# Value blocks multiplied in pairs, as products of 512 columns, for five token groups

## The chip, the cores and the metric

One core of a Trainium2 chip runs the whole layer as one program. The metric is the device time of that core in microseconds, the median of several executions. A profiled execution of the same program gives the rows below.

## The reference, cut to what matters

The input x has 2048 tokens of 1024 channels. A norm with shift and scale from the vector c gives h, and one product with `w_in` gives all projections:

```python
h = rmsnorm(h_res, norm_w[l]) * (1.0 + scale[:, None, :]) + shift[:, None, :]
proj = h @ w_in + b_in
(na_q, na_k, na_v, na_z, ml_q, ml_k, ml_v, ml_o, ml_z, i_f, f_f, i_b, f_b) = jnp.split(proj, split_idx, axis=-1)
```

`na_*` feed a neighbourhood attention on a 32 x 64 grid, `ml_*` a chunked mLSTM in both directions, with `ml_o` as its output gate. Both outputs are joined, multiplied by `w_out`, gated, added to x and normed.

## The kernel before

Every product is made of float32r parts: a weight and an activation are each split into a high and a low part, and three matmuls (high times high, high times low, low times high) for each of eight k tiles of 128 channels add up in one PSUM bank (`mm3`, L600 to L606). h lies split in SBUF as `hhi[g]` and `hlo[g]` for four groups of 512 tokens.

The columns of `w_in` are cut into blocks of 256 (`layout`). Blocks 0 to 3 hold the mLSTM's value and output gate of one head each, blocks 4 and 5 the attention's values, blocks 6 to 9 the mLSTM's keys and queries, the rest z, k and q. A block is loaded in two halves of four k tiles to the two `raw` buffers (`raw_w`, L198) and split into the high and low tiles of one of two slots, `wslot[0]` (whi_a, wlo_a) and `wslot[1]` (whi_b, wlo_b): ScalarE (ACT) copies raw to the high part (L208), VectorE (DVE) subtracts it from raw for the low part (L209), and for blocks over 2 the subtraction is ordered behind an eviction.

The stages come in this order. `start` (written out by hand, in fixed order) makes h and multiplies blocks 0 and 1 for all groups, and group 0 of block 2 from a third slot; its last steps load and split block 2 into slot 0, fill some tables in DRAM (`table_fills`, L721) and store the last results. `tok_blocks` (L738) multiplies groups 1 to 3 of block 2, then all four of blocks 3, 4 and 5: below, (2,1) is group 1 of block 2. A token tile has 128 tokens as the stationary operand (the columns of `hhi` or `hlo`) and a block's 256 columns as the moving one, so 24 matmuls of 128x256 to half a PSUM bank, of which four are in turn (`pp`). DVE adds the bias row and evicts to a stage tile (`vo_group` for blocks 0 to 3, L676; `nav_group` for 4 and 5, L639); for blocks 0 to 3 ACT then takes the sigmoid of the gate half (L682). The group's store on SP's queue (L687) is deferred and sent out after the second tile of the next group. Two stage tiles alternate. In block n the next block is loaded at once and split into the other slot after groups 1 and 2.

`tok_blocks` also drives a chain, one step after each eviction: first the gates of the mLSTM (`gate_chain`: small copies and scans on DVE, exponentials on ACT, transposes on PE through the one buffer of the PSUM pool `sp`), with a second generator for the residual's gate (`gate_row`: `ga` weights loaded by SP at L562, sums on DVE, two small products at L582), then the decay matrices (`decays`). Ahead of the first step `tables_begin` loads `rneg`, negates it on DVE (L694) and fills three tables `d_e` from SP. Outside the parts that are fixed by hand, the framework's scheduler orders the instructions of each engine by the program's order and its own model of time.

`conv_blocks` then multiplies blocks 6 to 9 with the weights stationary and 512 tokens moving (`pc`), the next blocks being split into the other slot. In phase 1b slot 0 serves the remaining projections (`pq`, L1046), spread among the mLSTM's two passes; slot 1's space is given back and the pools of that phase lie on it. The second pass loads a 128 x 769 chunk of `d_ck` into one of four `ck` tiles (L1253), and `weigh` (L1275) writes the weighted scores over the chunk's decay columns. Phase 2 is the attention and the output product; its score tables are loaded to four tiles `tab` (L1495), the first of them when the mLSTM ends.

```python
for g in range(1 if blk == 2 else 0, NG):
    if blk < 4:
        self.vo_group(blk, blk % 2, g)
    else:
        self.nav_group(blk, blk % 2, g)
    if g in (1, 2):
        parts[g - 1](self.nc.vector)
```

## Time and profile before

| | us |
|---|---|
| median of 3 runs (1303.35 to 1304.36) | 1304.31 |
| profiled execution, its own time | 1305.46 |
| its span, first to last instruction | 1303.7 |

In the rows, PE is TensorE's matmul, PEld its weight load, DVE VectorE, ACT ScalarE, POOL GpSimd, SPq the queue of SyncE, from which most transfers are issued. A row of the timeline has start, duration (us), engine, line, operation, out<-in, count, and in brackets the idle time before it with what ended it. Ends of matmuls are modelled, so starts are the safer measure. In a windows row, (x) is the count of instructions, and the last columns are PE's granted clock, the busy share of the 16 DMA engines and GB/s.

### The profile page before, as it was taken

To read this page: it belongs to the slowest core of one execution; us is meant where nothing else is said; L and a number is where in the kernel's file an instruction comes from. 1 tells how busy PE (TensorE), PEld (TensorE's weight loads), DVE (VectorE), ACT (ScalarE), POOL (GpSimd) and SP (SyncE) were. 2 spreads that over 40 slices of the span, in tenths; PEclk is the share of its full clock that TensorE was granted. 3 is DMA by queue.
4 is the path that set the end of the run, shared out by engine and by line. 5 is a ranking of instruction groups with operands and counts; after the bars stand their busy time and mean duration, and the time that the engine had idled before them with its cause. 6 is when DMAs were issued, how large, how long until landed. Compare 5 with 4: busy or idle time off the path is not lost.

```text
span 1303.7 us, 22944 instructions
## 1 busy us (share of the span) xinstructions
PE 1277.4 (98%) x8170; PEld 1103.3 (85%) x8170; DVE 794.7 (61%) x2384; ACT 532.3 (41%) x1172; POOL 258.6 (20%) x385
## 2 busy tenths in 40 slices
PE   9889999999999999999999999999999999999997
PEld 8889999999888887788888888888877878778776
DVE  5876353112567565166677877777657676767664
ACT  4444243543234222123333323333357555555551
POOL 1400002441000000102212002212224332332541
PEclk7989999999999999999999999999999999999999
DMA  9799955997678763745756767656688744655551
GB/s 365 260 293 295 254 195 136 253 234 193 189 179 197 173 153 97 202 122 161 198 164 201 246 195 220 211 176 169 201 252 276 225 156 154 201 179 171 169 167 66
DMA packets 217514, 259.08 MB, mean 199 GB/s; under 512 B 23867, under 2 KB 164027, under 8 KB 217400
## 3 DMA queue, kind: packets, MB, share of 16 engines
q1 hardware_dynamic: 142294, 186.48, 49.8%
q0 software_dynamic: 13616, 37.28, 9.1%
q10 hardware_dynamic: 61490, 33.85, 9.1%
q8 instruction: 65, 1.06, 0.3%
q14 instruction: 49, 0.40, 0.1%
HBM read 173.05 MB, written 92.72 MB: 204 GB/s over the span
## 4 chain that ended last, share of the span: by engine, by line
PE 77%; issue 5%; ACT 3%; DVE 3%; DMA 2%; POOL 1%; POOLq 0%; SPq 0%; ACTq 0%; DVEq 0%
PE pq L1046 24%; PE y L1611 7%; PE pc L605 4%; PE pc L606 4%; PE pc L604 4%; PE pvo L604 3%; PE pvo L606 3%; PE pvo L605 3%; PE pO L1568 3%; PE pT L1553 2%; PE pv L606 2%; PE pv L605 2%; PE pv L604 2%; PE pS L1522 2%; PE pi L1285 2%
## 5 line engine op out<-in xcount | busy, mean ns | idle before, releaser
L1046 PE MATMUL pq<-hhi,whi_a 128*128 128x512 f32 x512 | 208.3, 407 | 0.9 <-ACT u L951 0.9
L1046 PE MATMUL pq<-hlo,whi_a 128*128 128x512 f32 x512 | 208.3, 407 | 0.0
L1046 PE MATMUL pq<-hhi,wlo_a 128*128 128x512 f32 x512 | 207.1, 405 | 0.9 <-POOL wlo_a L1020 0.9
L1046 PEld LDWEIGHTS pq<-hhi,wlo_a 128*128 128x128 f32 x512 | 96.7, 189 | 17.6 <-POOL wlo_a L1020 1.3
L1046 PEld LDWEIGHTS pq<-hhi,whi_a 128*128 128x128 f32 x512 | 96.7, 189 | 17.4 <-ACT u L951 1.3
L1046 PEld LDWEIGHTS pq<-hlo,whi_a 128*128 128x128 f32 x512 | 96.8, 189 | 16.2 <-issue 0.6
L1020 POOL TENSOR_TENSOR wlo_a<-rawq,whi_a 128x1024 fp32r<-128x1024 f32 x19 | 45.5, 2395 | 295.8 <-ACT whi_a L1019 284.1
L1534 ACT ACTIVATE ring<-ring,mn 128x480 f32<-128x480 f32 (+5 forms) x128 | 76.0, 595 | 56.9 <-DVE mn L1533 56.6
L1555 ACT ACTIVATE ring<-pT 96x384 f32<-96x384 f32 (+3 forms) x128 | 65.6, 513 | 64.1 <-PE pT L1553 62.3
L1611 PE MATMUL y<-hhi,wlo_a 128*128 128x512 f32 (+1 forms) x272 | 89.7, 396 | 0.6 <-ACT y L1618 0.6
L1611 PE MATMUL y<-hhi,whi_a 128*128 128x512 f32 x256 | 88.6, 410 | 0.0
L1288 ACT ACTIVATE num<-px,gtile 128x129 f32<-128x129 f32 x120 | 38.3, 366 | 112.4 <-PE px L1283 83.7
L1460 POOL DMA_DIRECT2D v<-d_vna x158 | 79.0, 506 | 26.0 <-DMA v<-d_vna 6.3
L1307 POOL TENSOR_TENSOR hm<-hm,ck 128x128 f32<-128x128 f32 x64 | 27.5, 430 | 250.1 <-DVE hm L1306 213.8
L1553 PEld LDWEIGHTS pT<-ident,ring 128*128 128x128 f32 (+2 forms) x416 | 50.4, 136 | 26.9 <-ACT ring L1555 12.3
L1553 PE MATMUL pT<-ident,ring 128*128 128x128 f32 (+2 forms) x416 | 67.0, 274 | 3.9 <-ACT ring L1555 3.9
L1533 DVE CUSTOM_DVE_ANT_0 ring<-pS,tab 128x480 f32<-128x480 f32 (+5 forms) x128 | 62.4, 540 | 7.1 <-PE pS L1522 6.0
L604 PE MATMUL pvo<-whi_b,hhi 128*128 128x256 f32 x224 | 64.0, 286 | 0.5 <-DVE gates L678 0.5
L606 PE MATMUL pvo<-whi_b,hlo 128*128 128x256 f32 x224 | 63.2, 282 | 0.0
L605 PE MATMUL pvo<-wlo_b,hhi 128*128 128x256 f32 x224 | 63.2, 282 | 0.0
L893 ACT ACTIVATE dec<-dec,gtile 128x128 f32<-128x128 f32 x128 | 41.4, 391 | 46.9 <-POOL dec L886 36.6
L676 DVE TENSOR_TENSOR stvo<-pvo,brow 128x256 f32<-128x256 f32 x60 | 24.9, 420 | 58.3 <-PE pvo L606 43.4
(336 smaller groups left out, 3371.4 us busy)
## 6 DMA issues: line engine op xcount, KB each, us to landing
ck<-d_ck SPq DMA_DIRECT2D x64, 384.5 KB, 3.5
rawq<-in_w_main_dram SPq DMA_DIRECT2D x28, 512.0 KB, 4.5
raw<-in_w_main_dram SPq DMA_DIRECT2D x18, 512.0 KB, 5.8
kv<-d_ck SPq DMA_DIRECT2D x64, 128.5 KB, 3.2
dec<-d_mneg SPq DMA_DIRECT2D x32, 256.0 KB, 6.1
d_ck<-dec ACTq DMA_DIRECT2D x32, 256.0 KB, 6.6
d_ck<-stvo SPq DMA_DIRECT2D x15, 514.0 KB, 4.5
d_qna<-qst ACTq DMA_DIRECT2D x30, 256.0 KB, 4.5
```

The source lines that it names most:

```text
L604: nc.tensor.matmul(ps, lhi(k), rhi(k), start=(k == 0), stop=False)
L605: nc.tensor.matmul(ps, lhi(k), rlo(k), start=False, stop=False)
L606: self.mark = nc.tensor.matmul(ps, llo(k), rhi(k), start=False, stop=(k == KT - 1))
L893: nc.scalar.activation(t[:, o, :], t[:, o, :], AF.Exp, bias=self.cols["g"][:, d, h, c : c + 1])
L1020: (eng or nc.gpsimd).tensor_tensor(lo[:, :, cs], raw, hi[:, :, cs].bitcast(F32), ALU.subtract)
L1046: self.mark = nc.tensor.matmul(patch_ps(ps) if patch else ps, w, self.htok(h, g, k, patch), start=(k == 0 and n == 0), stop=(k == KT - 1 a ...
L1460: queue.dma_start(chunks[key][r * nkc : (r + 1) * nkc, :], rows[r])
L1533: nc.vector.tensor_tensor_reduce(pt[:, :nk], ps, tabs[ct][:, j * nk : (j + 1) * nk], 1.0, 3e38, ALU.add, ALU.min, mn)
L1534: nc.scalar.activation(pt[:, :nk], pt[:, :nk], AF.Exp, bias=mn, scale=-1.0, accum_out=sums[:, j : j + 1])
L1553: nc.tensor.transpose(ps[:cs, i, :], U[u][j][:, i * cs : (i + 1) * cs], self.ident)
L1555: nc.scalar.activation(t[:cs, :nch, :], ps[:cs, :nch, :], AF.Copy)
L1611: nc.tensor.matmul(y, m[:, k, :], w[k][:, cs], start=(k == 4 and n == 0), stop=(k == 3 and n == 2))
```

## The change

Both slots become one tile for the high and one for the low parts (`wpair`, 272 columns in each slot). For groups 2 and 3 of blocks 2 and 3, and groups 1 to 3 of blocks 4 and 5, `pair_group` multiplies both blocks at once: the moving operand takes 256 columns from each slot, 512 in all, into a whole PSUM bank, and two additions evict it to two stage tiles. The groups run in the order (2,1), (3,0), pair (2,2), pair (2,3), (3,1), (4,0), pairs (4,1), (4,2), (4,3), (5,0). Loads and splits get new places: block 3 is loaded ahead of the chain's first step and of `tables_begin` and split after the second and third tile of (2,1); block 4 is loaded then and split in (3,1), block 5 in (4,0), block 6 in (5,0). The chain takes one step for each addition, so two after a paired tile. There are four stage tiles in `tok_blocks`. Slot 1's space is kept for the whole run, and the four `ck` tiles and then the four `tab` tiles lie in it (`spare`); `weigh` writes to tiles of its own.

```diff
--- before.py
+++ after.py
@@ -148,10 +148,8 @@
         self.qst = self.pool(right, "qst", bufs=1, side="right")
         r1a = ExitStack()
         self.stages = [self.qst, self.pool(r1a, "stage", bufs=1, side="right")]
-        wb = self.pool(r1a, "wb", bufs=1, side="right")
-        self.wslot = []
-        for nm, pl in (("a", wa), ("b", wb)):
-            self.wslot.append(tuple(pl.tile([P, KT, 272 if nm == "a" else 256], F32R, name=f"w{part}_{nm}") for part in ("hi", "lo")))
+        self.wpair = tuple(wa.tile([P, 2, KT, 272], F32R, name=f"w{part}") for part in ("hi", "lo"))
+        self.wslot = [tuple(part[:, j] for part in self.wpair) for j in range(2)]
         toks = ExitStack()
         misc = self.pool(toks, "misc", bufs=1, side="right")
         self.brows = [misc.tile([P, 256], F32, name=f"brow{i}") for i in range(2)]
@@ -170,7 +168,11 @@
         self.tp = self.pool(ps1a, "tp", bufs=3, space=PSUM)
         self.sp = self.pool(ps1a, "sp", bufs=1, space=PSUM)
 
-        self.tok_blocks(self.pool(toks, "chain", bufs=1, side="right"))
+        chain_pool = self.pool(toks, "chain", bufs=1, side="right")
+        held, more = self.stages, self.pool(toks, "stage2", bufs=2, side="right")
+        self.stages = [*held, more, more]
+        self.tok_blocks(chain_pool)
+        self.stages = held
         toks.close()
 
         cvs = ExitStack()
@@ -188,8 +190,8 @@
             held.append(self.hpools[g].tile([P, KT, GT], F32R, tag=f"h{part}{g}", name=f"h{part}{g}"))
 
     def stage_tile(self, name):
-        self.stages.reverse()
-        return self.stages[1].tile([P, 1032], F32, tag="st", name=name).rearrange("p (o c) -> p o c", o=4)
+        self.stages.append(self.stages.pop(0))
+        return self.stages[-1].tile([P, 1032], F32, tag="st", name=name).rearrange("p (o c) -> p o c", o=4)
 
     def load_w(self, blk, slot, halves=(0, 1)):
         for part in self.raw_w(blk, slot, halves):
@@ -498,7 +500,7 @@
                 part(nc.vector)
 
         fills = self.table_fills()
-        self.chain = iter(())
+        self.chain = self.mid = iter(())
         for g in range(NG):
             now = [4 * g + j for j in range(4)]
             tiles = [tt + 4 for tt in now] if g < NG - 1 else []
@@ -631,17 +633,60 @@
 
     def nav_group(self, blk, slot, g):
         nc = self.nc
-        c0 = (blk - 4) * 256
         st = self.stage_tile(f"stv_{blk}_{g}")
         for o in range(4):
             ps = self.pp.tile([P, GT], F32, tag="pp", name=f"pv_{blk}_{g}_{o}")
             self.tok_tile(ps[:, :256], self.wslot[slot], 4 * g + o)
             self.evicted = nc.vector.tensor_add(st[:, o, :256], ps[:, :256], self.brows[blk % 2])
             next(self.chain, None)
+            next(self.mid, None)
             if o == 1:
                 self.flush()
-        dst = self.d_vna[g * GT : (g + 1) * GT, c0 : c0 + 256].rearrange("(o p) c -> p o c", p=P)
-        self.defer(lambda: nc.sync.dma_start(dst, st[:, :, :256]))
+        self.stored(blk, g, st)
+
+    def pair_group(self, blk, g):
+
+        nc = self.nc
+        sts = [self.stage_tile(f"st2_{blk + j}_{g}") for j in range(2)]
+        hi, lo = self.wpair
+        if blk < 4:
+            for st in sts:
+                nc.gpsimd.memset(st[:, :, 128:129], 1.0)
+        for o in range(4):
+            ps = self.pp.tile([P, GT], F32, tag="pp", name=f"p2_{blk}_{g}_{o}")
+            self.mm3(
+                ps.rearrange("p (a c) -> p a c", a=2),
+                lambda k: self.hhi[g][:, k, o * P : (o + 1) * P],
+                lambda k: self.hlo[g][:, k, o * P : (o + 1) * P],
+                lambda k: hi[:, :, k, :256],
+                lambda k: lo[:, :, k, :256],
+            )
+            for j, st in enumerate(sts):
+                row, part = self.brows[(blk + j) % 2], ps[:, 256 * j : 256 * j + 256]
+                if blk < 4:
+                    pair = st[:, o].rearrange("p (j c) -> p j c", j=2)[:, :, 0:128]
+                    self.evicted = nc.vector.tensor_add(pair, part.rearrange("p (j c) -> p j c", j=2), row.rearrange("p (j c) -> p j c", j=2))
+                else:
+                    self.evicted = nc.vector.tensor_add(st[:, o, :256], part, row)
+                next(self.chain, None)
+            next(self.mid, None)
+            if o == 1:
+                self.flush()
+        for j, st in enumerate(sts):
+            self.stored(blk + j, g, st)
+
+    def stored(self, blk, g, st):
+        nc = self.nc
+        if blk < 4:
+            nc.scalar.activation(st[:, :, 129:257], st[:, :, 129:257], AF.Sigmoid)
+            dst, src = self.d_ck[blk, 4 * g : 4 * g + 4, :, 128:385].rearrange("o p c -> p o c"), st[:, :, 0:257]
+        else:
+            c0 = (blk - 4) * 256
+            dst, src = self.d_vna[g * GT : (g + 1) * GT, c0 : c0 + 256].rearrange("(o p) c -> p o c", p=P), st[:, :, :256]
+        if g == 0 and blk < 3:
+            (nc.scalar if blk == 0 else nc.sync).dma_start(dst, src)
+        else:
+            self.defer(lambda: nc.sync.dma_start(dst, src))
 
     def load_bias(self, blk):
         self.nc.sync.dma_start(self.brows[blk % 2], self.b_row[0:1, 256 * blk : 256 * blk + 256].broadcast_to([P, 256]))
@@ -677,15 +722,10 @@
             if h == 0:
                 nc.vector.tensor_add(self.gates[:, :, tt], ps[:, 256:272], self.bgate)
             next(self.chain, None)
+            next(self.mid, None)
             if o == 1:
                 self.flush()
-        nc.scalar.activation(st[:, :, 129:257], st[:, :, 129:257], AF.Sigmoid)
-        dst = self.d_ck[h, 4 * g : 4 * g + 4, :, 128:385].rearrange("o p c -> p o c")
-        if g == 0 and h < 3:
-            (nc.scalar if h == 0 else nc.sync).dma_start(dst, st[:, :, 0:257])
-        else:
-            self.defer(lambda: nc.sync.dma_start(dst, st[:, :, 0:257]))
-
+        self.stored(h, g, st)
 
     def tables_begin(self, pool):
         nc = self.nc
@@ -738,20 +778,36 @@
     def tok_blocks(self, chain_pool):
         self.wide = chain_pool.tile([P, 2 * D], F32, name="wide")
         self.chain = itertools.chain(self.gate_both(chain_pool), self.decays(chain_pool))
-        order = [2, 3, 4, 5]
+        self.parts = self.raw_w(3, 1)
+        self.load_bias(3)
         next(self.chain)
         self.tables_begin(chain_pool)
-        for n, blk in enumerate(order):
-            parts = self.raw_w(blk + 1, (blk + 1) % 2)
-            if blk < 5:
-                self.load_bias(blk + 1)
-            for g in range(1 if blk == 2 else 0, NG):
-                if blk < 4:
-                    self.vo_group(blk, blk % 2, g)
-                else:
-                    self.nav_group(blk, blk % 2, g)
-                if g in (1, 2):
-                    parts[g - 1](self.nc.vector)
+        order = [(2, 1), (3, 0), (2, 2), (2, 3), (3, 1), (4, 0), (4, 1), (4, 2), (4, 3), (5, 0)]
+        both = ((2, 2), (2, 3), (4, 1), (4, 2), (4, 3))
+
+        def splits(rest, after):
+            for _ in range(rest):
+                yield
+            for part in self.parts:
+                part(self.nc.vector)
+                yield
+            if after:
+                self.parts = self.raw_w(*after)
+                if after[0] == 5:
+                    self.load_bias(4)
+                if after[0] == 6:
+                    self.load_bias(5)
+
+        turns = {0: (1, (4, 0)), 4: (0, (5, 1)), 5: (0, (6, 0)), 9: (0, None)}
+        for n, (blk, g) in enumerate(order):
+            group = self.vo_group if blk < 4 else self.nav_group
+            self.mid = splits(*turns[n]) if n in turns else iter(())
+            if (blk, g) in both:
+                self.pair_group(blk, g)
+            else:
+                group(blk, blk % 2, g)
+            for _ in self.mid:
+                pass
         for _ in self.chain:
             pass
         self.flush()
@@ -1119,6 +1175,7 @@
         self.owed = 0
         self.zdone = set()
         self.norms, self.turns, self.ends, self.stores = [], [], [], []
+        self.cks = itertools.count()
         kk = self.kk_jobs()
         self.jobs = kk[0] + kk[1] + kk[2] + kk[3]
         passes = []
@@ -1136,6 +1193,10 @@
         mls.close()
         self.todo = []
         self.stacks = [pps, right, left]
+
+    def spare(self, i, n):
+        part = self.wslot[1][i // 2].rearrange("p a b -> p (a b)").bitcast(F32)
+        return part[:, i % 2 * 1088 : i % 2 * 1088 + n]
 
     def close(self):
 
@@ -1249,7 +1310,7 @@
         qk, vo, mb, sc, hm, mv, stage, zt = {}, {}, {}, {}, {}, {}, {}, {}
 
         def load(c):
-            t = ml.tile([P, 769], F32, tag="ck", bufs=4, name=f"ck_{h}_{c}")
+            t = self.spare(next(self.cks) % 4, 769)
             nc.sync.dma_start(t, self.d_ck[h, c, :, 128:897])
             vo[c] = t[:, 0:257]
             qk[c] = t[:, 257:513].rearrange("p (j t) -> p j t", j=2)
@@ -1272,7 +1333,8 @@
 
         def weigh(c):
             m = mb[c]
-            nc.vector.scalar_tensor_tensor(m, sc.pop(c).unsqueeze(1).broadcast_to([P, 2, CH]), KSCALE, m, ALU.mult, ALU.mult)
+            mb[c] = ml.tile([P, 2, CH], F32, tag="wm", bufs=3, name=f"wm_{h}_{c}")
+            nc.vector.scalar_tensor_tensor(mb[c], sc.pop(c).unsqueeze(1).broadcast_to([P, 2, CH]), KSCALE, m, ALU.mult, ALU.mult)
 
         def combine(c):
             s, q, v = mb.pop(c), qk.pop(c)[:, 0, :], vo[c]
@@ -1488,7 +1550,7 @@
             L[b]["x"] = [x[:, 512 * i : 512 * i + 512] for i in range(2)]
             L[b]["row"] = x
 
-        tabs = [p.tile([P, 960], F32, name=f"tab{i}") for i in range(4)]
+        tabs = [self.spare(i, 960) for i in range(4)]
 
         def load_tab(b, ct, queue=nc.sync):
             src = self.d_t[PR_T[b // 4]][PC_T[b % 4]][ct].rearrange("q e k -> q (e k)")
```

## Rows read from the trace of the kernel before

**Rows 1.** The page's first part: busy us, share of the span, instructions of each engine.

```profile
PE 1277.4 (98%) x8170; PEld 1103.3 (85%) x8170; DVE 794.7 (61%) x2384; ACT 532.3 (41%) x1172; POOL 258.6 (20%) x385
```

**Rows 2.** PE's waits, the longest line: us in total, times, longest.

```profile
PE pT L1553 <- ACT ring L1555: 3.9, 15, 1.0
```

**Rows 3.** Windows: busy us of each engine in 150 to 200 us.

```profile
150.00:200.00 50.00, 50.00 (x412) 48.29 (x411) 27.70 (x75) 16.43 (x20) 0.53 (x5) 1.00 0.69 204
```

**Rows 4.** Timeline of PE: first products of block 5 and of the convolution.

```profile
276.77 0.28 PE L604 MATMUL pv<-whi_b,hhi 128*128 128x256 f32 x1
...
322.33 0.39 PE L604 MATMUL pc<-hhi,whi_a 128*128 128x512 f32 x1
```

**Rows 5.** Timeline of PE in the convolution: two products, 84 from one to the other.

```profile
324.44 0.39 PE L604 MATMUL pc<-hhi,whi_a 128*128 128x512 f32 x1
...
343.90 0.39 PE L604 MATMUL pc<-hhi,whi_a 128*128 128x512 f32 x1
```

**Rows 6.** Windows: products of line 1046 alone in 510 to 530 us.

```profile
510.00:530.00 20.00, 20.00 (x88) 16.19 (x87) 1.00 0.64 148
```

**Rows 7.** Timeline of PE around group (2,1).

```profile
146.96 0.28 PE L604 MATMUL pvo<-whi_a,hhi 128*128 128x256 f32 x1
...
149.79 0.27 PE L773 MATMUL ps_gi<-ident,wide 128*128 128x128 f32 x1
...
150.72 0.33 PE L773 MATMUL ps_gf<-ident,wide 128*128 128x128 f32 x1
...
158.58 0.28 PE L604 MATMUL pvo<-whi_a,hhi 128*128 128x256 f32 x1
```

**Rows 8.** Timeline of ACT: copies that split block 2's second half and block 3.

```profile
143.83 1.06 ACT L208 ACTIVATE whi_a<-raw 128x1024 fp32r<-128x1024 f32 x1 [0.19 <-DMA raw<-in_w_main_dram]
...
162.80 1.06 ACT L208 ACTIVATE whi_b<-raw 128x1024 fp32r<-128x1024 f32 x1 [9.12 <-DMA raw<-in_w_main_dram]
...
166.01 1.06 ACT L208 ACTIVATE whi_b<-raw 128x1024 fp32r<-128x1024 f32 x1 [0.20 <-DMA raw<-in_w_main_dram]
```

**Rows 9.** Timeline of SP's queue, 132 to 160 us.

```profile
132.82 1.53 SPq L562 DMA_DIRECT2D ga<-in_w_gt_dram  x3
...
141.36 0.38 SPq L687 DMA_DIRECT2D d_ck<-stvo  x1
141.78 4.38 SPq L721 DMA_DIRECT2D d_t<-big  x2
148.38 3.89 SPq L687 DMA_DIRECT2D d_ck<-stvo  x1
...
157.07 0.63 SPq L204 DMA_DIRECT2D raw<-in_w_main_dram  x1
```

**Rows 10.** Timeline of DVE: block 2's second subtraction.

```profile
145.15 1.21 DVE L209 TENSOR_TENSOR wlo_a<-raw,whi_a 128x1024 fp32r<-128x1024 f32 x1
```

**Rows 11.** Windows: 143.8 to 162.8 us.

```profile
143.80:162.80 19.00, 19.00 (x161) 18.55 (x160) 9.59 (x26) 4.89 (x7) 0.21 (x2) 1.00 1.05 265
```

**Rows 12.** DMA issues, KB each, us to landing: 140 to 163 us, then the page.

```profile
d_t<-big SPq DMA_DIRECT2D x1, 1440.0 KB
d_t<-big SPq DMA_DIRECT2D x1, 1152.0 KB, 14.6
...
raw<-in_w_main_dram SPq DMA_DIRECT2D x18, 512.0 KB, 5.8
...
d_ck<-stvo SPq DMA_DIRECT2D x15, 514.0 KB, 4.5
```

**Rows 13.** Timeline of POOL, last read of ck; the tile tab's first reader.

```profile
926.91 0.41 POOL L1307 TENSOR_TENSOR hm<-hm,ck 128x128 f32<-128x128 f32 x1 [3.40 <-DVE hm L1306]
...
L1533 DVE CUSTOM_DVE_ANT_0 ring<-pS,tab x128: 426/527/659, 949.6 to 1259.3; 128x360 f32<-128x360 f32 x32, 128x480 f32<-128x480 f32 x32, 128x288 f32<-128x288 f32 x16, 128x264 f32<-128x264 f32 x16
```

**Rows 14.** Timeline of DVE: rneg and the evictions after it.

```profile
159.03 0.18 DVE L694 TENSOR_SCALAR rneg<-rneg 120x31 f32<-120x31 f32 x1 [4.06 <-DMA rneg<-in_rpb_dram]
...
161.51 0.76 DVE L676 TENSOR_TENSOR stvo<-pvo,brow 128x256 f32<-128x256 f32 x2
```

## The prediction

> **What bounds the kernel now.** Begin with the page's first part [rows 1]: TensorE (PE) is busy for 98% of the span. Then PE's waits, line by line [rows 2]: the reader should see how small even the longest is, 3.9 us in 15 pieces, and that it lies in a late stage. A window of the stage that the change rewrites, which runs from 146.96 to 322.33 us, says the same [rows 3]: PE is busy for all of its 50 us, at a granted clock of 1.00. So in this stage the end is set by how many matmuls PE does and how long each keeps it. A shorter product shortens the run one for one; a wait in front of PE lengthens it one for one, since nothing later has slack on PE to absorb it.
>
> A busy matmul overlaps its neighbour, so I take a price from start to start. Block 5 begins at 276.77 and the convolution's first product at 322.33 [rows 4]. Between them lie 16 tiles of 24 products of 256 columns: 45.56/384 = 118.6 ns each. For 512 columns, two rows of the convolution with 84 products from one to the other give (343.90 - 324.44)/84 = 231.7 ns [rows 5].
>
> **The products.** The five paired groups have 20 tiles. They remove 20 x 48 = 960 products of 256 columns and add 480 of 512: 113.9 us at 118.6 ns go, 111.2 us at 231.7 ns come. That is **2.6 us** less. PE already works nearly by the column, so a pair has only 237.2 - 231.7 = 5.5 ns to give.
>
> No row shows a moving operand in two runs of 256 columns that lie a slot apart. The nearest is the later patch product, whose moving operand is regrouped into runs of 16 columns: 88 of 0.39 us each touch a window of 20 us, (20 + 0.39)/88 = 231.7 ns again [rows 5, 6]. So I take no extra. The dear end is the first nine wide products after the narrow ones, (324.44 - 322.33)/9 = 234.4 ns [rows 4, 5]; by that the gain is 480 x 2.8 ns = 1.3 us. For a better price than 231.7 no row gives a reason.
>
> [...]
>
> The 480 weight loads that go cost nothing now: they run under the products, busy beside a full PE [rows 3]. The evictions stay 40 additions of some 0.4 us; two now follow one tile of 5.56 us, and four PSUM buffers cover them. Without that cover a tile would cost 0.8 us more. The chain takes as many steps as before, two after each wide tile, and its small products on PE stay.
>
> **The earlier split of block 3.** This is the term that can eat the gain. Before, block 2 ran three groups alone, and block 3's weights were wanted only after them. Now (2,1) alone stands in front of (3,0), which reads slot 1. (2,1) starts at 146.96, and its 96 products and two transposes end at 158.58 [rows 7]. The first half of block 3's weights (k 0 to 3) must be split by then, the second 12 products or 1.4 us later, at 160.0. In the trace the first copy of that split starts at 162.80 and the second at 166.01, both after a wait for the load [rows 8]. Left there, with 1.06 us for the copy and 1.2 for the subtraction [rows 8, 10], the halves would be ready at 165.1 and 168.3 and PE would stand some 8 us. So it depends on how far the load comes forward.
>
> SP's queue [rows 9] shows what the load stood behind: a store to d_ck at 141.36, two table fills at 141.78, another store at 148.38, and then gate weights, rneg and the d_e fills of tables_begin. The change puts block 3's loads and bias ahead of the last three, but the fills and the first store belong to the start and stay ahead. The raw buffers come free with block 2's subtractions, the second at 145.15 + 1.21 = 146.4 [rows 10]; SP is on the fills until 146.16. So the loads go out at about 146.4.
>
> When would they land? From 143.8 (block 2's second half is just in [rows 8]) to 162.8 (block 3's first half) the DMA engines were full, at a share of 1.05 and 265 GB/s [rows 11]. That first half, 0.52 MB, took 5.7 us from its issue at 157.07, where it needs 2.0 at this rate: it waited its turn behind older transfers. So I let them drain in order. In the new order the store (514 KB), the fills (1152 and 1440) and the first half (512) [rows 12] are 3.70 MB and end at 143.8 + 14.0 = 157.8, the second half 2.0 us later. The halves are ready at 160.1 and 162.1: PE waits 1.5 us and then 0.6, **2.1 us** in all. That is one end of the ordinary case. The other is nothing: three loads of gate weights that went out at 132.82, ahead of block 2's, may now come behind; then the queue is empty when the store goes out at 141.36, and the halves are ready at 141.4 + 14.0 + 2.3 = 157.7 and 159.7, both in time. I take **1.0 us**, between the two, since one row speaks for each.
>
> Block 4's loads follow block 3's split and are wanted some 45 us later: no cost. Block 5's can go out after block 4's subtractions in (3,1), near 219 and 222; the median load of this kind lands in 5.8 us [rows 12], so by 228, and the pair (4,1) begins near 237. No cost; those 9 us are the cover.
>
> **Later stages.** The d_ck chunks and the first score tables now live in slot 1's space, so the tables wait for the last reader of a chunk, at 926.91; the first operation that reads a table comes at 949.6 [rows 13]. 22 us cover the load: nothing. weigh writes a new tile instead of in place, the same operation: nothing.
>
> **The sum.** -2.6 + 1.0 = -1.6 us. The profiled execution took 1305.46 (its span 1303.7), 1.15 over the median of 1304.31; against itself that is 1303.9, against the median **1302.7 us**. About 0.2%, 2.6 us, is what a measurement of this kernel can tell from no change.
>
> **Rivals.**
> - No wait at all: -2.6, 1301.7. For it, the order of issue in the program; against it, the full DMA queues.
> - Slower: the second subtraction of block 3 stands behind rneg on VectorE (DVE). In the trace DVE stood 4.06 us until rneg landed at 159.03, with the gate chain queued behind it, so that two evictions came only at 161.51 [rows 14]. Now rneg's load has another 1.05 MB ahead of it, 4.0 us: 163.0. With the 2.5 us of chain steps behind it and its own 1.2 the subtraction ends at 166.7, where 160.0 was wanted: 6.7 us, net +4.1, 1308.4. It decides if rneg's operation is put ahead of that subtraction and lands after 158.9, from where the wait is over 2.6. Against it: the subtraction is tied to the third tile's eviction at about 155.5, and its load goes out first.
>   [...]
> - Little gain from the width: 1.3 comes in and the 2.1 us of waiting stays, +0.8, 1305.1. If products of 512 cost 237.2 ns, the change does nothing of what its pairing says.
> - Chain steps in pairs: a second transpose or gate sum right behind the first must wait for the one PSUM buffer they share. In the trace two transposes stand 0.93 us apart with seven products between them [rows 7]; four such places without products are at most 3.7 us, net +2.1, 1306.4. Against it: that the seven products are there.
>
> **How the numbers follow.** The forecast, some wait of up to 2.1 us: 0.37, no difference. No wait: 0.30, most of it counted beyond 2.6 us, since small waits in the stage may also go. Rneg: 0.15, slower. Little gain from the width: 0.08, no difference. Chain pairs, or a wait in a later stage that I don't see: 0.10, half of it slower. So faster 0.27, same 0.53, slower 0.20. The range runs from 1300.6 (no wait, and 1 us of small waits gone) to 1308.0, just short of the rneg case.
>
> **What would show it.** Right: paired products 231 to 233 ns apart; a gap before (3,0) of under 2.1 us, ended by the split of slot 1; no waits from (3,1) on; the convolution starting 0.5 to 2.6 us before 322.33. Wrong: paired products at 237 ns or more; a gap of over 4 us near 160 us with DVE waiting for rneg; PE waiting for slot 1 before (4,1); or a convolution that starts earlier and an end that doesn't follow, which would put the loss in the shared space.

## The result, and the profile after

The changed kernel takes **1308.26 us** (median of 20 runs, 1304.6 to 1312.84), the kernel before in the same comparison 1304.34 (20 runs, 1302.47 to 1312.05). The ratio is **1.0024 [1.0013, 1.0035]**: slower, where no difference was forecast, and 0.3 us above the range.

The stage of the change is read best from the first transpose of (2,1), ps_gi, to the first product of the convolution, pc: what comes ahead of it differs by several us from run to run. Before, it lasts 322.33 - 149.79 = 172.5 us [rows 4, 7]; after, 322.19 - 146.51 = 175.7. The pairs should have taken 2.6 us out, and 3.1 came in. The two rows of after:

```profile
146.51 0.27 PE L829 MATMUL ps_gi<-ident,wide 128*128 128x128 f32 x1
...
322.19 0.40 PE L606 MATMUL pc<-hhi,whi 128*128 128x512 f32 x1
```

The page's first part, after: PE has 480 instructions fewer [rows 1] and 3.0 us less of busy time, in a span 4.7 us longer.

```profile
PE 1274.4 (97%) x7690; PEld 1075.5 (82%) x7690; DVE 795.2 (61%) x2384; ACT 532.4 (41%) x1172; POOL 257.4 (20%) x385
```

PE's waits, after (us in total, times, longest). The longest line of before [rows 2] is still first; new are the waits for whi and wlo at lines 606 and 607 and one for chunks of d_ck in phase 1b.

```profile
PE pT L1615 <- ACT ring L1617: 3.2, 15, 0.6
...
PE pvo L606 <- ACT whi L210: 2.8, 1, 2.8
PE a L1331 <- DMA whi<-d_ck: 2.7, 2, 2.2
...
PE pvo L607 <- DVE wlo L211: 0.9, 1, 0.9
```

The timeline of PE, after, where (2,1) ends and (3,0) begins:

```profile
155.18 0.28 PE L608 MATMUL pvo<-whi,hlo 128*128 128x256 f32 x1
158.28 0.38 PE L606 MATMUL pvo<-whi,hhi 128*128 128x256 f32 x1 [2.82 <-ACT whi L210]
159.53 0.58 PE L607 MATMUL pvo<-wlo,hhi 128*128 128x256 f32 x1 [0.88 <-DVE wlo L211]
159.92 0.42 PE L608 MATMUL pvo<-whi,hlo 128*128 128x256 f32 x1
160.13 0.41 PE L606 MATMUL pvo<-whi,hhi 128*128 128x256 f32 x1
```

At 118.6 ns a product the first was due at 155.30 and the second at 158.40: 2.98 + 1.13 = **4.1 us** of standing. Behind it the products are 0.21 us apart and not 0.119. Windows of the same stretch show why (busy us of PE, PEld, DVE, ACT, POOL, then the granted clock, DMA share, GB/s): the clock, 1.00 in the kernel before [rows 3], falls to 0.50.

```profile
156.00:158.00 2.00, 0.00 (x0) 0.00 (x0) 0.00 (x0) 0.83 (x1) 0.00 (x0) 1.00 0.99 334
158.00:160.00 2.00, 0.85 (x3) 0.65 (x4) 1.75 (x3) 1.28 (x2) 0.00 (x0) 0.82 1.10 364
160.00:162.00 2.00, 2.00 (x11) 2.00 (x11) 2.00 (x5) 0.52 (x1) 0.00 (x0) 0.50 0.40 122
162.00:164.00 2.00, 2.00 (x16) 1.84 (x15) 0.89 (x3) 1.97 (x3) 0.00 (x0) 0.83 0.52 145
164.00:166.00 2.00, 2.00 (x17) 1.75 (x16) 1.87 (x12) 0.72 (x1) 0.00 (x0) 1.00 0.80 229
```

What PE waited for: the timelines of ACT (block 3's two copies), DVE (the two subtractions, then rneg) and SP's queue, after.

```profile
157.16 1.06 ACT L210 ACTIVATE whi<-raw 128x1024 fp32r<-128x1024 f32 x1 [6.78 <-DMA raw<-in_w_main_dram]
158.51 1.06 ACT L210 ACTIVATE whi<-raw 128x1024 fp32r<-128x1024 f32 x1 [0.29 <-DMA raw<-in_w_main_dram]
```

```profile
158.25 1.23 DVE L211 TENSOR_TENSOR wlo<-raw,whi 128x1024 fp32r<-128x1024 f32 x1 [4.28 <-ACT whi L210]
...
159.73 1.22 DVE L211 TENSOR_TENSOR wlo<-raw,whi 128x1024 fp32r<-128x1024 f32 x1
160.86 0.17 DVE L734 TENSOR_SCALAR rneg<-rneg 120x31 f32<-120x31 f32 x1
```

```profile
138.52 0.38 SPq L689 DMA_DIRECT2D d_ck<-stvo  x1
138.94 5.07 SPq L761 DMA_DIRECT2D d_t<-big  x2
145.08 4.06 SPq L689 DMA_DIRECT2D d_ck<-stvo  x1
149.24 2.60 SPq L206 DMA_DIRECT2D raw<-in_w_main_dram  x2
```

So the split was waiting for the load, and the load stood behind the last store to d_ck, whose issue took 4.06 us. It came in 7.9 us after its own issue.

The rest of the 4.7 us by which the two profiles differ is not the stage's: the transpose came 3.3 us earlier, the stage is 3.1 longer, the stretch from the first score to the last inner product of the mLSTM's second pass (a to pi) 6.1 longer, and the stretches between and behind make up -1.2.

### The profile page after: what moved, and what is told of

It reads as the page before. It is cut to its first block, busy times and chain, and to the rows that moved or that the text cites. A ratio compares the mean times of both kernels' runs of the same rounds, so it can differ in the third digit from the quotient of the medians.

```text
span 1308.4 us, 22003 instructions
## 1 busy us (share of the span) xinstructions
PE 1274.4 (97%) x7690; PEld 1075.5 (82%) x7690; DVE 795.2 (61%) x2384; ACT 532.4 (41%) x1172; POOL 257.4 (20%) x385
## 5 line engine op out<-in xcount | busy, mean ns | idle before, releaser
L1102 PE MATMUL pq<-hhi,whi 128*128 128x512 f32 x512 | 208.1, 406 | 0.9 <-ACT u L1007 0.9
L1102 PE MATMUL pq<-hlo,whi 128*128 128x512 f32 x512 | 208.6, 407 | 0.0
L1102 PE MATMUL pq<-hhi,wlo 128*128 128x512 f32 x512 | 207.4, 405 | 0.2 <-POOL wlo L1076 0.2
L1102 PEld LDWEIGHTS pq<-hhi,whi 128*128 128x128 f32 x512 | 96.8, 189 | 17.7 <-ACT u L1007 1.3
L1102 PEld LDWEIGHTS pq<-hhi,wlo 128*128 128x128 f32 x512 | 96.8, 189 | 16.7 <-POOL wlo L1076 0.7
L1102 PEld LDWEIGHTS pq<-hlo,whi 128*128 128x128 f32 x512 | 96.8, 189 | 16.3 <-issue 0.6
L606 PE MATMUL pc<-hhi,whi 128*128 128x512 f32 x256 | 101.8, 398 | 0.0
L607 PE MATMUL pc<-hlo,whi 128*128 128x512 f32 x256 | 101.6, 397 | 0.0
L608 PE MATMUL pc<-hhi,wlo 128*128 128x512 f32 x256 | 100.5, 393 | 0.0
L1673 PE MATMUL y<-hhi,wlo 128*128 128x512 f32 (+1 forms) x272 | 89.5, 396 | 0.7 <-ACT y L1680 0.7
```

What stands on the lines that cost most here:

```text
L606: nc.tensor.matmul(ps, lhi(k), rhi(k), start=(k == 0), stop=False)
L607: nc.tensor.matmul(ps, lhi(k), rlo(k), start=False, stop=False)
L608: self.mark = nc.tensor.matmul(ps, llo(k), rhi(k), start=False, stop=(k == KT - 1))
L1102: self.mark = nc.tensor.matmul(patch_ps(ps) if patch else ps, w, self.htok(h, g, k, patch), start=(k == 0 and n == 0), stop=(k == KT - 1 a ...
L1673: nc.tensor.matmul(y, m[:, k, :], w[k][:, cs], start=(k == 4 and n == 0), stop=(k == 3 and n == 2))
```

## The experiments

One table for all; gi is the start of that transpose, then the two stretches, in us, of the profiled execution. Each ratio is to runs of the kernel before on the same chip. The expectations of the first four experiments count the stage from the first product of (2,1), 2.8 us ahead of that transpose: their 175.4 is 172.5 here, their 178.5 is 175.7.

| run | median us | ratio [95%] | gi | gi to pc | a to pi |
|---|---|---|---|---|---|
| before | 1304.34 | | 149.8 | 172.5 | 348.3 |
| after | 1308.26 | 1.0024 [1.0013, 1.0035] | 146.5 | 175.7 | 354.3 |
| e1_space_alone | 1305.33 | 1.0006 [0.9991, 1.002] | 150.7 | 172.4 | 349.5 |
| e2_load_first | 1303.91 | 0.9999 [0.9984, 1.0013] | 152.0 | 170.1 | 348.6 |
| e3_narrow_pairs | 1312.65 | 1.0063 [1.0047, 1.0079] | 148.6 | 178.5 | 350.1 |
| e4_after_again | 1310.17 | 1.0042 [1.0025, 1.006] | 152.1 | 177.3 | 352.2 |
| e5_filler | 1309.97 | 1.0016 [1.0002, 1.0031] | 149.2 | 174.0 | 351.1 |
| e6_two_alone | 1304.15 | 0.9983 [0.9972, 0.9995] | 148.9 | 170.5 | 350.4 |
| e7_first_again | 1304.51 | 0.9986 [0.9971, 1.0001] | 146.8 | 170.8 | 351.8 |
| e8_before_again | 1305.57 | 1.0001 [0.9984, 1.0017] | 147.3 | 172.5 | 349.4 |
| e9_load_middle | 1310.13 | 1.0036 [1.0023, 1.0049] | 146.4 | 175.2 | 350.3 |
| e10_two_and_first | 1305.89 | 1.0 [0.9986, 1.0015] | 151.7 | 171.5 | 349.3 |
| e11_two_again | 1303.72 | 0.9999 [0.9983, 1.0015] | 149.8 | 170.5 | 350.2 |

**The shared space by itself.** The kernel before, in its old order, with one tile for both slots, chunks and tables in slot 1's space, and weigh writing a new tile:

```diff
+        self.wpair = tuple(wa.tile([P, 2, KT, 272], F32R, name=f"w{part}") for part in ("hi", "lo"))
+        self.wslot = [tuple(part[:, j] for part in self.wpair) for j in range(2)]
...
-            t = ml.tile([P, 769], F32, tag="ck", bufs=4, name=f"ck_{h}_{c}")
+            t = self.spare(next(self.cks) % 4, 769)
...
-        tabs = [p.tile([P, 960], F32, name=f"tab{i}") for i in range(4)]
+        tabs = [self.spare(i, 960) for i in range(4)]
```

> The kernel before with one part of the change alone: both slots in one tile, slot 1 kept for the whole run, the ck and tab tiles in it, and weigh writing to a tile of its own; no pairs, the old order, loads and splits. Theory 1 (the shared space makes the mLSTM stage longer): 4 to 6 us over the kernel before, and from the first score product a to the first pS some 379 us as in the profile of after, where before had 373. Theory 2 (that stage scatters from run to run, and the shared space is not at fault): within 1.5 us of before. On both theories the stretch from group (2,1) to the convolution stays 175.4 us.

1.0006 [0.9991, 1.002], and the stage 172.4; from the first a to the first pS it took 374.6 us, nearer the 373 of before than the first theory's 379. No loss that this run can measure in the total, and none in the stage: there it is in the order or the pairs.

**The load ahead of the fills.** The changed kernel with block 3's load put ahead of the last table fills:

```diff
@@ start
+        self.parts = self.raw_w(3, 1)
         for _ in fills:
             pass
         self.flush()
@@ tok_blocks
-        self.parts = self.raw_w(3, 1)
         self.load_bias(3)
```

> The changed kernel with the two loads of block 3 issued ahead of the last two table fills and of the last store of the start, nothing else moved. Theory 1 (PE's wait ahead of (3,0) and the half clock behind it are all that the first stage loses): no wait over 0.5 us there, granted clock 1.00 from 150 to 200 us, from (2,1) to the convolution 172.7 us (175.4 less 2.6) instead of 178.5, and 5 to 6 us less than the changed kernel. Rival (the load only makes room for something else that is late, such as the fills, the stores or the gate chain): the wait moves to another place in the stage, and less than half of the 5.8 us comes back.

The stage falls to 170.1, 2.4 under before and 5.6 under after. SP's queue in this run: the two loads go out between smaller issues, and now the fills of d_t and the store behind them are the long rows. The framework put rneg, a gate weight and two of the d_e fills ahead with them; the sixth experiment leaves the queue's order alone.

```profile
146.53 0.36 SPq L206 DMA_DIRECT2D raw<-in_w_main_dram  x1
146.94 1.60 SPq L740 DMA_DIRECT2D d_e<-big  x2
148.64 0.58 SPq L206 DMA_DIRECT2D raw<-in_w_main_dram  x1
149.26 5.17 SPq L762 DMA_DIRECT2D d_t<-big  x2
154.54 4.91 SPq L690 DMA_DIRECT2D d_ck<-stvo  x1
```

Its window of 150 to 200 us is full again, at a clock of 1.00; after had 46.30 busy us there at 0.97.

```profile
150.00:200.00 50.00, 50.00 (x313) 43.97 (x312) 25.94 (x72) 16.00 (x20) 0.32 (x3) 1.00 0.71 204
```

So all that the stage lost is the wait for this load and what follows from it. The median is 6.3 us under that of the changed kernel on the same chip (fourth experiment).

**The pairs as narrow products.** The changed kernel, but a pair is computed as two times 256 columns:

```diff
-            self.mm3(
-                ps.rearrange("p (a c) -> p a c", a=2),
...
-            )
+            for j in range(2):
+                self.tok_tile(ps[:, 256 * j : 256 * j + 256], self.wslot[(blk + j) % 2], 4 * g + o)
```

> The changed kernel with its order, loads, stores and space, but each paired tile computed as two runs of 24 products of 256 columns into the two halves of the bank. Theory 1 (the wide product earns 5.4 ns a pair, 480 times): 2.6 us more than the changed kernel, from (2,1) to the convolution 181.1 us. Rival (the width earns nothing): no difference from the changed kernel.

The cleanest reading is the three pairs of block 4, with no wait in them. In the timeline of PE they run, wide (after) and then narrow (this run), from the first row of p to the first of pv:

```profile
244.11 0.40 PE L606 MATMUL p<-whi,hhi 128*128 128x512 f32 x1
...
310.86 0.28 PE L606 MATMUL pv<-whi,hhi 128*128 128x256 f32 x1
```

```profile
247.57 0.28 PE L606 MATMUL p<-whi,hhi 128*128 128x256 f32 x1
...
315.73 0.28 PE L606 MATMUL pv<-whi,hhi 128*128 128x256 f32 x1
```

66.75/288 = 231.8 ns for 512 columns, 68.16/576 = 118.3 for 256: 4.9 ns a pair, **2.35 us** for all 480. The width earns what was forecast, within 0.3 us. The whole run is at 1.0063 [1.0047, 1.0079], its median 2.5 us over that of the changed kernel on the same chip. Its stage is 2.8 us over after's: 2.35 by the width, 0.7 because the clock was at 0.50 for longer, from 160 to 166 us, less 0.3 of standing.

**The changed kernel again**, on the chip of the first three:

> The changed kernel once more, beside the others on one chip. From (2,1) to the convolution 178.5 us with a wait of 4.1 us ahead of (3,0) on every theory. From the first a to the first pS: 379 us if the shared space is at fault, anything from 373 to 380 if that stage scatters. Total 3 to 4 us over before.

1.0042 [1.0025, 1.006]; PE stood 3.5 and 0.7 us in front of (3,0), the granted clock was 0.50 from 166 to 170 us, and the stage took 177.3. The loss is there each time. By the starts PE stood 4.8 us, 0.7 more than after, and the longer half clock cost another 0.7.

**Filler in the wait.** 24 products in front of (3,0) that nobody reads:

```diff
+            if n == 1:
+                self.tok_tile(self.pp.tile([P, GT], F32, tag="pp", name="idle")[:, :256], self.wslot[0], 4)
             if (blk, g) in both:
```

> The changed kernel with 24 more products of 256 columns (block 2's weights, result never read) put between (2,1) and (3,0), so that PE works 2.8 us of the time in which it stood. Theory (of the 5.8 us lost at (3,0) some 4.0 are waiting for the split and the rest is PE's half clock after the wait): the filler itself costs nothing, no granted clock of 0.5 behind it, (3,0) runs from its first to its last product in 12.4 to 12.8 us where it took 14.7, and from the first transpose of (2,1) to the convolution 173.9 to 174.3 us, where the changed kernel took 175.7. Rival (it is all waiting, the clock costs nothing): 175.7 as before, or more if the split is late by less than the filler takes.

The stage took 174.0, inside the theory's 173.9 to 174.3. The window behind the filler, as above:

```profile
160.00:162.00 2.00, 1.39 (x12) 1.18 (x11) 1.60 (x3) 1.43 (x2) 0.00 (x0) 1.00 1.02 330
162.00:164.00 2.00, 2.00 (x19) 2.00 (x18) 2.00 (x5) 0.37 (x1) 0.00 (x0) 1.00 0.32 102
```

PE was kept busy, and the clock stayed at 1.00. (3,0) ran from 160.79 to 174.03, 13.2 us where 12.4 to 12.8 were expected and 14.7 measured after. The stage is 1.6 us shorter than after's, but not all of that is the clock: the load also came in sooner in this run, and the second product of (3,0), which waits for the first subtraction, started 12.5 us behind the transpose, where after it was 13.0. That leaves 1.1. (3,0) without its inner waits of 0.88 and 0.61 gives 1.2, and its first tile from the second product to the last, 4.12 us after and 2.75 here, gives 1.4. So the half clock cost **1.1 to 1.4 of the 5.6 us**, the standing itself some 4.1.

**More work in front of the wait.** (2,1) and (2,2) alone ahead of (3,0), four pairs in place of five, the load where the change has it:

```diff
-        order = [(2, 1), (3, 0), (2, 2), (2, 3), (3, 1), (4, 0), (4, 1), (4, 2), (4, 3), (5, 0)]
-        both = ((2, 2), (2, 3), (4, 1), (4, 2), (4, 3))
+        order = [(2, 1), (2, 2), (3, 0), (2, 3), (3, 1), (3, 2), (4, 0), (4, 1), (4, 2), (4, 3), (5, 0)]
+        both = ((2, 3), (4, 1), (4, 2), (4, 3))
...
-        turns = {0: (1, (4, 0)), 4: (0, (5, 1)), 5: (0, (6, 0)), 9: (0, None)}
+        turns = {1: (1, (4, 0)), 4: (0, (5, 1)), 6: (0, (6, 0)), 10: (0, None)}
```

> The changed kernel with (2,1) and (2,2) alone in front of (3,0), block 3 split during (2,2), and four paired groups in place of five. The load keeps its late place in SP's queue but has 11.4 us more. Theory (the loss is only that the load is late by some 4 us): no wait at (3,0), granted clock stays 1.0, 4 x 0.53 = 2.1 us gained in the stage, 170.4 us from the first transpose to the convolution (172.5 before), total 1302.5 to 1304.5 and 4 to 6 us under the changed kernel. Rival (the pairs or the stretch of the mLSTM in phase 1b lose time whatever stands before (3,0)): the total stays at 1307 or more.

0.9983 [0.9972, 0.9995], the stage 170.5 where 170.4 was expected, the median 1304.15, and PE full again:

```profile
150.00:200.00 50.00, 50.00 (x346) 45.12 (x345) 26.14 (x73) 13.67 (x17) 0.42 (x4) 1.00 0.61 183
```

Four pairs without the wait are worth 172.5 - 170.5 = 2.0 us in the stage. Of the versions tried this is the one to keep.

**The early load with more runs**, with the edit of the second experiment:

> The changed kernel with block 3's load ahead of the last stores and table fills of the start, as in the second experiment, once more and with more runs. Theory (the pairs gain 2.6 us in their stage, and the time follows): ratio to before 0.9975 to 0.9985. Rival (some 1 to 2.5 us come back elsewhere, from the shared space or a later start): 0.9985 to 1.0005; then the profile's stretches beside those of before show where.

0.9986 [0.9971, 1.0001]: on the border of the two, and the stage 170.8, with one wait of 0.5 us for the second half's subtraction.

**The kernel before, a second profile:**

> The kernel before, unchanged: a second profile, for how far its stretches scatter by themselves. Theory (the stage of the change is steady, the start and the mLSTM stretch scatter): first transpose to convolution 172.3 to 172.7 us again, start of that transpose anywhere from 146 to 152 us, first score to last inner product of the second mLSTM pass 348 to 354 us. Rival (the stretches are steady): 149.8 and 348.3 within 0.5 us, and the 352 and 354 us of the changed kernel are the change's own.

The stage is steady, 172.5 again (172.8 and 173.5 in the two later profiles, where PE waited 0.2 and 0.9 us for the chain's `ends`). The start scatters, by 2.5 us here and from 146.4 to 152.4 over all profiles. The mLSTM's stretch came 1.1 us longer, less than the theory allowed it.

**The order that the prediction had assumed.** Block 3's load between the last fills and the last store:

```diff
@@ start
         for _ in fills:
             pass
+        self.parts = self.raw_w(3, 1)
         self.flush()
@@ tok_blocks
-        self.parts = self.raw_w(3, 1)
         self.load_bias(3)
```

> The changed kernel with block 3's load between the last table fills of the start and the last store to d_ck: the order that the prediction had assumed. Theory (the load was late because SP held the issue of that store, 4.06 us in the changed kernel's profile, and the load stood behind it): the load goes out 4 us earlier, the waits at (3,0) shrink from 2.8 and 0.9 to between 0 and 1 us, the granted clock stays at 1.0, first transpose to convolution 170 to 171.5 us, time 4 to 6 us under the changed kernel and a ratio to before of 0.998 to 1.000. Rival (the fills fill the DMA queues, and the load lands when they have drained, wherever it stands): waits of 2 us or more together and the half clock behind them, 174 us or more, ratio over 1.001.

The theory failed: 175.2 us and 1.0036 [1.0023, 1.0049]. SP's queue: the store is short now, and the held time has passed to the loads.

```profile
138.64 5.08 SPq L762 DMA_DIRECT2D d_t<-big  x2
143.82 6.08 SPq L206 DMA_DIRECT2D raw<-in_w_main_dram  x2
150.00 0.58 SPq L690 DMA_DIRECT2D d_ck<-stvo  x1
```

ACT and the two subtractions on DVE in this run:

```profile
154.38 1.06 ACT L210 ACTIVATE whi<-raw 128x1024 fp32r<-128x1024 f32 x1 [5.69 <-DMA raw<-in_w_main_dram]
155.46 1.28 ACT L844 ACT_TABLE_LOAD   x1
156.75 0.31 ACT L844 ACTIVATE wide<-wide 128x128 f32<-128x128 f32 x1
156.97 1.04 ACT L210 ACTIVATE whi<-raw 128x1024 fp32r<-128x1024 f32 x1
```

```profile
155.47 1.23 DVE L211 TENSOR_TENSOR wlo<-raw,whi 128x1024 fp32r<-128x1024 f32 x1 [5.33 <-ACT whi L210]
...
158.82 1.23 DVE L211 TENSOR_TENSOR wlo<-raw,whi 128x1024 fp32r<-128x1024 f32 x1
```

The transposes of this run and of after lie 0.08 us apart, so the times compare directly: the load went out 5.4 us earlier, the first copy began 2.8 us earlier and the second 1.5. The second half now came behind a step of the gate chain on both engines: on ACT a table load and an exponential, on DVE five small operations and an eviction. PE's waits in the stage:

```profile
PE pvo L608 <- DVE wlo L211: 2.5, 2, 1.6
PE ps_ends L867 <- DVE ends L864: 1.5, 1, 1.5
```

That is 4.1 us in three pieces, and the granted clock stayed at 1.00: behind the first piece, 0.87 us in front of a product at 156.75, the products start 0.12 us apart from 156.98 on. By the starts, as for after above, it is 1.4 us for the first half, 1.8 for the second and 1.7 for the chain, together **5.0**, and 172.5 - 2.35 + 5.0 is the stage's 175.2. The rival, that the fills delay the load wherever it stands behind them, holds; the half clock that it also expected did not come.

**Both remedies together**, the edits of the second and the sixth experiment:

> (2,1) and (2,2) alone as in the sixth experiment, and block 3's load ahead of the last stores and fills as in the second. Theory (either edit alone removes the whole wait): nothing more to gain, 170.3 to 170.7 us from the first transpose to the convolution and a ratio to before within 0.001 of the sixth experiment's 0.9983. Rival (a part of the loss was still there in the sixth, as waits behind the split): under 170.0 us and a ratio of 0.997 or less. If the early load costs the stores and fills that now stand behind it, 171 us or more.

Nothing more to gain: 1.0 [0.9986, 1.0015], and a stage of 171.5 us, outside the theory's 170.3 to 170.7 and in the last case, the early load that costs the store behind it. PE has one wait of 0.8 us for a subtraction. Ahead of that subtraction DVE stood for a store to d_ck:

```profile
168.14 0.43 DVE L722 TENSOR_TENSOR stvo<-pvo,brow 128x256 f32<-128x256 f32 x1 [3.62 <-DMA d_ck<-stvo]
```

The last store of the start now stands behind the fills and the load, and its issue took 5.18 us. So the trace speaks for that case, though it is one profile.

**The sixth experiment again:**

> The sixth experiment's kernel once more: (2,1) and (2,2) alone, four paired groups, block 3's load in its late place. Theory (2.0 us of the stage are gained and nothing takes them back): no wait of PE between the first transpose of (2,1) and the convolution, 170.3 to 170.7 us for that stretch, ratio to before 0.9975 to 0.9992. Rival (the sixth experiment's ratio was a lucky draw of the start and of the mLSTM stretch, as the tenth's 1.0 suggests): the stretch is the same, but the ratio lies at 0.9995 or more.

The stage is 170.5 again, without a wait, but the ratio 0.9999 [0.9983, 1.0015], as the rival had it. By medians from different chips the two runs are 4.1 to 6.5 us under the changed kernel; against the kernel before, one comparison shows a gain and one doesn't.

**Does the shared space lose time in the mLSTM's stretch?** The kernels without the wait for the load gain 1.0 to 2.4 us in the stage, by their ratios between nothing and 2.2. Two more profiles of the kernel before and one of the shared space alone:

> The kernel before, a look at its mLSTM stretch (first score to last inner product of the second pass): 348.3 and 349.4 us so far, with 2.5 and 3.2 us of waits of PE in it. Theory (the shared space costs some 1 to 2 us there, in small waits): 348 to 350 again. Rival (the stretch only scatters): anything up to 352.

> As the twelfth: 348 to 350 us by the theory, anything up to 352 by the rival.

> The shared space alone once more (349.5 us and 3.6 us of waits in the first experiment). Theory (the shared space costs 1 to 2 us there): 349.5 to 352. Rival (it costs nothing): 348 to 350 like the kernel before.

Measured: 349.9 and 350.8 for the kernel before, 349.8 for the shared space. So before has 348.3 to 350.8 in four profiles, the shared space alone 349.5 and 349.8, the five profiles with the change and without the wait for the load (e2, e6, e7, e10, e11) 348.6 to 351.8. The groups don't part, and the rival holds as far as so few profiles can tell: a cost of under 1 us would not show in them.

## Why the prediction was wrong

**Right.** The pairs: 231.8 ns where 231.7 was taken, and 2.35 to 2.4 us of the 2.6. The shared space, weigh's new tile, block 4's and block 5's loads: no waits in the stage from (3,1) on, and no time that the first experiment could measure. The moving operand in two runs cost nothing: 231.8 ns a product, where the convolution's in one run took 231.7 [rows 5]. The rival of little gain from the width falls with it.

**The step that failed** is "The earlier split of block 3", taken as 1.0 us between ends of 0 and 2.1. By the second experiment it cost 5.6. Three things in it:

- *"SP is on the fills until 146.16. So the loads go out at about 146.4."* They went out at 149.24 of a run whose transpose is 3.3 us earlier, 152.5 on the axis of before: the last store was ahead, and its issue took 4.06 us. The prediction names this store, at 148.38, and then leaves it out of what stays ahead, though `start` ends with it; the row was there, an issue of 3.89 us [rows 9]. Nor is that the store's own: the issue right behind the fills is long, be it a store (3.06 to 5.66 us in 15 profiles; 3.89 before [rows 9], 4.06 after, 4.91 in the second run) or a load (4.91 of the ninth run's 6.08 for two). The load ahead of the fills came in time (second run, no wait of PE in the stage), and the load behind them late, with the store ahead of it (after, 4.1 us of standing) or not (ninth run, 5.0).
- *The halves one after the other.* With the order as assumed (ninth experiment, moved by the 3.36 us between the transposes) the halves were ready at 160.06 and 163.41; the prediction had 160.1 and 162.1. So the drain of the fills was priced right, to 0.1 us on the first half. The second half was 1.3 us late, because both ACT and DVE put steps of the chain between the halves, which the prediction had left out, and PE then waited 1.55 us for the ends of that chain. By the starts the dear end was not 1.5 + 0.6 = 2.1 but 1.4 + 1.8, and 1.7 for the chain: 5.0.
- *"a wait in front of PE lengthens it one for one"*: it did more. The products after the wait ran at half the clock, granted 0.50 and 0.21 us apart where 0.119 is usual in this stage. In the changed kernel's profile that cost 1.1 to 1.4 us more, and in the third and the fourth run 2.1, by the same first tile (4.86 us, where behind the filler it took 2.75). This too was in the trace of before, in a stage that the prediction didn't read. There PE stood 3.57 us in front of a product at 71.17, and the row and the windows from 66 us on are

```profile
71.17 0.59 PE L659 MATMUL pvo<-whi_a,hhi 128*128 128x272 f32 x1 [3.57 <-ACT hhi L397]
```

```profile
66.00:68.00 2.00, 1.60 (x14) 1.39 (x12) 0.00 (x0) 0.00 (x0) 0.00 (x0) 1.00 0.60 187
68.00:70.00 2.00, 0.00 (x0) 0.00 (x0) 1.38 (x4) 0.00 (x0) 0.11 (x1) 0.90 0.09 18
70.00:72.00 2.00, 0.83 (x3) 0.83 (x4) 1.87 (x4) 1.61 (x3) 0.00 (x0) 0.50 1.08 293
72.00:74.00 2.00, 1.94 (x8) 1.62 (x8) 2.00 (x4) 1.23 (x3) 0.10 (x1) 0.50 0.99 270
74.00:76.00 2.00, 2.00 (x10) 2.00 (x10) 1.86 (x4) 2.00 (x5) 0.00 (x0) 0.50 0.95 320
76.00:78.00 2.00, 2.00 (x17) 2.00 (x16) 1.87 (x4) 2.00 (x5) 0.00 (x0) 0.89 1.02 412
```

  So the clock was at 0.50 behind a gap of 3.57 us here, whose wait was for ACT, behind 2.82 and 0.88 in the changed kernel, 2.53 and 0.68 in the third run and 3.52 and 0.68 in the fourth; behind the three waits of the ninth, 0.87, 1.65 and 1.55 us, it stayed at 1.00.

**The rivals.** rneg did not come between: both subtractions ran ahead of it, at 158.25 and 159.73 before 160.86. The slower side came true through the place that the forecast itself had named, the load, at a price that no case held. That the rneg case was priced at 1308.4, beside the measured 1308.26, is chance. Chain steps in pairs did not show: in the stage after, PE has no other wait of 0.2 us or more. The sum by what was measured is -2.4 + 4.1 + 1.4 = +3.1 us, and the stage shows 3.1.

**Left open.** Both profiles of the changed kernel also lost 2 us in the mLSTM's stretch in one wait for a chunk (2.2 and 2.1 us), and had the two longest times of all, 354.3 and 352.2; no other profile waits there over 0.7. Whether that is chance isn't settled. Over the ten comparisons of kernels with pairs, the total (by the ratio) lies on average 1.1 us above what the stage accounts for, from -0.2 to 2.3; the shared space alone shows 1.0, with an interval almost 2 us to either side. So some 1 us may be lost outside the stage, and no run shows where. The start's scatter of 6 us is larger than what is asked for. Pairs with chunks and tables in tiles of their own were not tried.

## What to carry to other kernels

Before a load is called earlier, follow it through the queue that issues it: here the issue right behind two large fills took 3.1 to 5.7 us, and one place forward in the program was worth less (0.5 us of the stage) than one more group of work ahead of its reader (5.2). A wait of PE can cost more than the standing: here waits of 3.2 to 4.2 us had the half clock (granted 0.50) behind them. Look for such a gap elsewhere in the same trace and price it from there. A gain of 2 us of 1300 is proven in its stage, not by the total.

## What the runs showed of the hardware

- The clock fell to 0.50 behind standing of 3.2 (third run), 3.7 (after) and 4.2 us (fourth run) with one product between the two pieces, not behind 0.87, 1.65 and 1.55 with more products between them. How long it stayed there doesn't follow the wait: behind the shortest it was 0.50 from 160 to 166 us, behind 3.7 from 160 to 162 alone, with 0.82 and 0.83 on either side.
- With 24 products for nothing in the wait (fifth run) the clock stayed at 1.00 from 160 to 164 us, and the stage was 1.6 us shorter, 0.5 of it by an earlier load.
- The issue right behind the two fills of 1152 and 1440 KB took 3.06 to 5.66 us of SP's queue, whether it was a store of 514 KB or a load of 512 KB.
- One instruction order started its stage anywhere in 5 us: the four profiles of the kernel before have the transpose at 149.8, 147.3, 152.4 and 152.2 us.
